# QKV projection on one Trainium2 core: the weight blocks of the first two row pairs in halves of K, and one x load at another place in ScalarE's order

## The chip, the cores and the metric

The kernel runs on one core of one Trainium2 chip. The metric is the device time of one execution in microseconds (us), the median of several executions. A profile is one execution recorded by the hardware profiler. Five engines work side by side[...]: PE (TensorE, matmuls; its weight loads are shown as PEld), DVE (VectorE), ACT (ScalarE), POOL (GpSimd) and SP (SyncE, which here only issues DMAs). SPq and ACTq are the DMA-issuing instructions of SP and ACT.

## The reference

```python
batch, seq, hidden = 16, 512, 768          # x: 16 x 512 x 768, w_qkv: 768 x 2304, fp32
qkv = np.matmul(x, w_qkv)                  # 8192 x 768 times 768 x 2304
q, k, v = qkv[..., :768], qkv[..., 768:1536], qkv[..., 1536:]
return np.stack([q, k, v], axis=0)         # 3 x 16 x 512 x 768, fp32
```

So it is one matrix product of 8192 rows with K = 768, cut into three outputs by columns.

## The kernel before

**Tiling.** The 8192 rows are taken in 32 pairs p = 0..31 of two row tiles of 128 rows (r = 0, 1). K = 768 is six slices of 128 (KT = 6), in two halves of three slices (KH = 3). The 2304 columns are five groups: two quads q = 0, 1 of two blocks c = 0, 1 of 512 columns (CB), and a remainder of 256 columns (`rem`, `w_rem`). All instructions stand in an order written out by hand: each engine runs its own instructions in the order in which the code emits them.

**Pairs 2 to 31** (`two`) use a scheme of the Strassen kind. For a quad, seven products of half the size replace eight. Products 1 and 2 are bf16 (`b1`, rows from `xb`), products 3 to 7 use fp32r sums of w (`t1` to `t4`, and the copy `b22`) and of x (`sr`, made on POOL by `sums_x`). The sums of w are made by DVE in `sum_w(q, n)`, once for each quad. `do(u, n)` multiplies product n and evicts it on ACT or adds it on DVE. In a pair the order on PE is: product 1 of both quads (a, b), then a2, a6, b2, b6, a5, a7, b5, b7, a4, rem, b4, a3, b3. Product 6 accumulates into the PSUM bank of product 1, so it can start only when ACT has evicted product 1 of that quad into its output tile `o`.

`early()`, in the middle of each pair, makes the next pair's operands: `transpose(p+1)` on DVE, `round_x` and `sums_x` on POOL, and the x load of pair p+2. `load_x(p, halves)` is four DMAs of 192 KB: half 0 is issued by SP (two of them), half 1 by ACT (two).

**Pairs 0 and 1** can't use the scheme yet, because the sums of w aren't made. They are multiplied directly, in bf16, block by block: `block(q, c, w, then)` runs over four row tiles n and calls `direct`, six matmuls that accumulate over all of K, then an eviction on ACT. Behind the evictions of n = 0 and of n = 1 the hook `then` puts the two casts (fp32 to bf16, ACT, one for each half of K) of the next block of w. The first block's halves are cast by DVE and ACT. The four blocks follow each other: (q, c) = (0,0), (0,1), (1,0), (1,1), with bf16 tiles `b1[0]`, `bt0`, `b1[1]`, `bt1`. `busy(n)` are matmuls on zeros that keep PE occupied during the head.

**Loads.** SP issues, in this order: rows of pair 0, w of the remainder (`str`), rows of pair 1, the blocks of quad 0 (`load_blocks(0, 0)` and `(0, 1)`: one DMA of 1536 KB each, fp32 tiles `st0`), half 0 of x of pair 2, the blocks of quad 1 (two DMAs of 768 KB for each, tiles `st1`), half 0 of x of pair 3. After that come the stores. ACT issues half 1 of x of pair 2 behind the first cast of `b1[0]`, and half 1 of x of pair 3 behind the evictions of block (0,0). A pool of eight large tiles (`big_pool`) holds first `str` and the four `st1` halves and later the output tiles `o`: an output tile of pair 2 comes free when the last reader of the `st1` half that lay there has finished. For quad 0 of pair 2 that reader is `sum_w(1, 1)`, for quad 1 it is `sum_w(1, 4)`.

The order on DVE in the head is: casts of the first rows, a half of `w_rem`, half a cast of `b1[0]`, `sum_w(0,1)`, `sum_w(0,2)`, `transpose(2)`, `sum_w(0,3)`, `sum_w(0,4)`, `b22[0]`, `sum_w(1,1)` to `sum_w(1,4)`, `b22[1]`, `transpose(3)`, and then the additions of pair 2.

Every DMA counts up one of eight completion semaphores, dealt out in turn; a DMA is issued only when the one before it on the same semaphore has landed.

Of the kernel before, what the change touches and what calls it, by code (L numbers as in the profile page):

```python
# [10 lines left out]
def kernel(  # L11
# [20 lines left out]
    nc = tc.nc  # L32
    P = 128
# [5 lines left out]
    KT = K // P  # L39
    KH = KT // 2  # L40
    KC = K // 4
    NP = M // (2 * P)
    CB = 512
    REM = N3 - 4 * CB
    Q_OFF = (0, 2 * CB + REM)
    R_OFF = 2 * CB
# [3 lines left out]
    ident = mybir.ActivationFunctionType.Identity  # L50
# [28 lines left out]

    def load_w(dst, j0, nj, off, cols):  # L80
        rows = w_qkv.rearrange("(p j) n -> p j n", j=KT)
        nc.sync.dma_start(dst[:], rows[:, j0:j0 + nj, off:off + cols])  # L82

    stage = {}

    def load_blocks(q, c):
        if q == 0:
            t = tq_pool.tile([P, KT, CB], fp32, name="st0", tag="tq")
            load_w(t, 0, KT, Q_OFF[q] + c * CB, CB)
            stage[q, 0, c], stage[q, 1, c] = t[:, :KH, :], t[:, KH:, :]  # L90
        else:
            for h in range(2):
                t = big_pool.tile([P, KH, CB], fp32, name="st1", tag="big")
                load_w(t, h * KH, KH, Q_OFF[q] + c * CB, CB)
                stage[q, h, c] = t[:]

    def sum_w(q, n):
# [9 lines left out]
    xin, xf, xb, sr = {}, {}, {}, {}  # L107
# [3 lines left out]
    def load_x(p, halves=(0, 1)):  # L111
        if p not in xin:
            xin[p] = xin_pool.tile([P, 2 * P // G, KC], fp32, name="xin")
        t = xin[p]
        rows = x_flat[p * 2 * P:(p + 1) * 2 * P, :].rearrange("(g b) k -> b g k", b=G)
        for n in range(2):
            for h in halves:
                i = 2 * h + n
                eng = (nc.sync, nc.scalar)[h]
                eng.dma_start(t[i * G:(i + 1) * G], rows[:, :, i * KC:(i + 1) * KC])  # L120
# [10 lines left out]
    def load_rows(p):  # L131
        xin[p] = xin_pool.tile([P, 2, K], fp32, name="xin")
        rows = x_flat[p * 2 * P:(p + 1) * 2 * P, :]
        nc.sync.dma_start(xin[p][:], rows.rearrange("(r m) k -> m r k", m=P))  # L134
# [37 lines left out]
    def quad(p, q):  # L172
        u = Quad()
        u.p, u.q = p, q
        u.o = big_pool.tile([P, 2, 2 * CB], fp32, name="o", tag="big")
        u.x = u.y = u.z = None
        return u
# [17 lines left out]
    def bank():  # L195
        return ps_pool.tile([P, CB], fp32, name="ps")
# [29 lines left out]
    def rows_of(s, p, lo, hi):  # L226
        return out_flat[s, p * 2 * P:(p + 1) * 2 * P, lo:hi].rearrange("(r m) n -> m r n", m=P)

    def store_quad(u):
        if u.q == 0:  # L230
            nc.sync.dma_start(rows_of(0, u.p, 0, H), u.o[:, :, :H])
            nc.sync.dma_start(rows_of(1, u.p, 0, 2 * CB - H), u.o[:, :, H:])
        else:
            part = 2 * H - Q_OFF[1]
            nc.sync.dma_start(rows_of(1, u.p, H - part, H), u.o[:, :, :part])
            nc.sync.dma_start(rows_of(2, u.p, 0, H), u.o[:, :, part:])
# [13 lines left out]
        nc.scalar.activation(o[:], ps[:], ident)  # L250
        nc.sync.dma_start(rows_of(1, p, R_OFF - H, R_OFF - H + REM), o[:])

    def direct(p, r, c, o, w):

        ps = bank()
        for j in range(KT):
            nc.tensor.matmul(  # L257
                ps[:], xb[p][:, j, r * P:(r + 1) * P], w[:, j, :],
                start=(j == 0), stop=(j == KT - 1),
            )  # L260
        nc.scalar.activation(o[:, r, c * CB:(c + 1) * CB], ps[:], ident)

    def two(a, b, early):

        do(a, 1)
        do(b, 1)
        early()
        do(a, 2)
        do(a, 6)
        do(b, 2)  # L270
        do(b, 6)
        do(a, 5)
        do(a, 7)
        do(b, 5)
        do(b, 7)
        do(a, 4)
        rem(a.p)
        do(b, 4)
        do(a, 3)
        store_quad(a)  # L280
        do(b, 3)
        store_quad(b)
# [49 lines left out]
    eye = w_pool.tile([P, P], fp32, name="eye")  # L332
    make_identity(nc, eye)
    st_rem = big_pool.tile([P, KT, REM], fp32, name="str", tag="big")
    load_w(st_rem, 0, KT, R_OFF, REM)
    load_rows(1)
    load_blocks(0, 0)
    load_blocks(0, 1)
    load_x(2, (0,))
    o0 = [quad(p, 0) for p in range(2)]  # L340
    load_blocks(1, 0)
    load_blocks(1, 1)
    load_x(3, (0,))
    o1 = [quad(p, 1) for p in range(2)]
# [7 lines left out]
    def cast(q, h, c, w, eng):  # L352

        dst = w[:, h * KH:(h + 1) * KH, :]
        if eng is nc.scalar:
            eng.activation(dst, stage[q, h, c], ident)  # L356
        else:
            eng.tensor_copy(out=dst, in_=stage[q, h, c])

    def block(q, c, w, then):  # L360

        for n in range(4):
            p, r = divmod(n, 2)
            direct(p, r, c, (o0, o1)[q][p].o, w)
            if c == 1 and r == 1:
                store_quad((o0, o1)[q][p])
            then(n)

    act, dve = nc.scalar, nc.vector
    busy(8)  # L370
# [11 lines left out]
    bt1 = bt_pool.tile([P, KT, CB], bf16, name="bt")  # L382
# [8 lines left out]

    def cast_next(q, c, w):

        return lambda n: n < 2 and cast(q, n, c, w, act)

    block(0, 0, b1[0], cast_next(0, 1, bt0))
    load_x(3, (1,))
    block(0, 1, bt0, cast_next(1, 0, b1[1]))
    block(1, 0, b1[1], cast_next(1, 1, bt1))
    block(1, 1, bt1, lambda n: None)  # L400
    t_1 = [tq_pool.tile([P, 2, KH, CB], f32r, name=f"t_1{n}", tag="tq") for n in range(2)]
    ts[1] = [t_1[n // 2][:, n % 2] for n in range(4)]
    for n in range(1, 5):
# [46 lines left out]
```

## Time and profile before

| what | us |
|---|---|
| device time, median of 5 runs (372.35 to 375.2) | 372.7 |
| device time of the profiled execution | 373.14 |
| span in the profile, first to last instruction | 371.4 |
| of the execution outside the span (373.14 - 371.4) | 1.7 |
| PE busy | 358.9 (97%) |
| DVE busy | 229.8 (62%) |
| ACT busy | 185.5 (50%) |
| POOL busy | 183.8 (50%) |
| start of pair 2 on PE | 39.86 |
| time of one pair from there on (54 matmuls) | 10.87 |

The busy time of PE is an average: from 39.86 us to the end PE has work all the time, and before that it waits several times. So the head, the first 40 us, has to be read by itself: the chain of work that ended last says what was on the path, the timeline of one engine shows each instruction with the wait ahead of it in brackets, and the view of waits adds them up. Landing times of the DMAs below are the last of the sixteen completion marks that the trace has for each DMA.

### The profile page before, as it was taken

To read this page: it belongs to the slowest core of one execution; us is meant where nothing else is said; L and a number is where in the kernel's file an instruction comes from. 1 tells how busy PE (TensorE), PEld (TensorE's weight loads), DVE (VectorE), ACT (ScalarE), POOL (GpSimd) and SP (SyncE) were. 2 spreads that over 40 slices of the span, in tenths; PEclk is the share of its full clock that TensorE was granted. 3 is DMA by queue.
4 is the path that set the end of the run, shared out by engine and by line. 5 is a ranking of instruction groups with operands and counts; after the bars stand their busy time and mean duration, and the time that the engine had idled before them with its cause. 6 is when DMAs were issued, how large, how long until landed. Compare 5 with 4: busy or idle time off the path is not lost.

```text
span 371.4 us, 5137 instructions
## 1 busy us (share of the span) xinstructions
PE 358.9 (97%) x1776; PEld 246.4 (66%) x1776; DVE 229.8 (62%) x227; ACT 185.5 (50%) x303; POOL 183.8 (50%) x186
## 2 busy tenths in 40 slices
PE   7887999999999999999999999999999999999994
PEld 4533566777676677767667766767776666777673
DVE  2289985556667555666655576664657666556732
ACT  3487554544445455444444544445454445545442
POOL 0019475665435566544456654445665444665510
PEclk9999999999999999999999999999999999999999
DMA  7999968899888899988888998888998988899776
GB/s 286 350 326 328 371 199 298 276 302 314 290 269 286 287 282 301 319 287 272 281 295 274 304 322 279 275 282 285 284 312 297 293 276 287 286 288 312 256 265 246
DMA packets 80906, 108.09 MB, mean 291 GB/s; under 512 B 4720, under 2 KB 60912, under 8 KB 80880
## 3 DMA queue, kind: packets, MB, share of 16 engines
q1 hardware_dynamic: 63984, 95.17, 78.6%
q10 hardware_dynamic: 16896, 12.59, 10.9%
q8 instruction: 14, 0.23, 0.3%
q14 instruction: 12, 0.10, 0.1%
HBM read 32.24 MB, written 75.50 MB: 290 GB/s over the span
## 4 chain that ended last, share of the span: by engine, by line
PE 89%; DMA 8%; SPq 1%; ACT 1%; issue 0%; ACTq 0%
PE ps L190 77%; PE ps L240 11%; DMA st<-in_w_qkv_dram 8%; PE ps L257 1%; ACT bt L356 0%; SPq L82 0%; SPq L134 0%; ACT orem L322 0%; ACTq L324 0%
## 5 line engine op out<-in xcount | busy, mean ns | idle before, releaser
L190 PE MATMUL ps<-t,s 128*128 128x512 f32 x720 | 194.4, 412 | 0.0
L190 PEld LDWEIGHTS ps<-t,s 128*128 128x128 f32 x720 | 133.1, 188 | 32.4 <-ACT o L217 0.4
L153 POOL CAST xb<-xf 128x1536 bf16<-128x1536 f32 x30 | 45.3, 1511 | 167.3 <-DVE xf L124 159.8
L124 DVE STREAM_TRANSPOSE xf<-xin 128x1536 f32<-128x1536 f32 x30 | 90.0, 3001 | 3.7 <-DMA xin<-in_x_dram 3.6
L190 PE MATMUL ps<-b,xb 128*128 128x512 bf16 x360 | 88.1, 381 | 0.0
L224 DVE TENSOR_TENSOR o<-o,ps 128x512 f32<-128x512 f32 x60 | 41.3, 688 | 61.7 <-PE ps L190 61.6
L218 DVE TENSOR_TENSOR o<-o,ps 128x512 f32<-128x512 f32 x60 | 41.2, 688 | 54.0 <-ACT o L217 54.0
L190 PEld LDWEIGHTS <-xb 128*128 128x128 bf16 x360 | 30.5, 98 | 44.5 <-issue 15.2
L217 ACT ACTIVATE o<-ps 128x512 f32<-128x512 f32 x60 | 35.9, 598 | 46.8 <-PE ps L190 46.8
L204 ACT ACTIVATE o<-ps 128x512 f32<-128x512 f32 x60 | 35.8, 597 | 44.7 <-PE ps L190 40.8
L211 ACT ACTIVATE o<-ps 128x512 f32<-128x512 f32 x60 | 35.9, 599 | 44.0 <-PE ps L190 43.9
L240 PE MATMUL ps<-w_rem,xb 128*128 128x256 bf16 x384 | 47.5, 273 | 1.0 <-DVE w_rem L373 1.0
L190 PE MATMUL ps<-b,s 128*128 128x512 f32 x180 | 46.5, 393 | 0.0
L240 PEld LDWEIGHTS <-xb 128*128 128x128 bf16 x384 | 35.2, 98 | 13.0 <-issue 9.4
L190 PEld LDWEIGHTS ps<-b,s 128*128 128x128 f32 x180 | 33.8, 188 | 8.0
L208 DVE TENSOR_TENSOR o<-o,ps 128x512 f32<-128x512 f32 x60 | 37.7, 671 | 2.0 <-PE ps L190 2.0
L221 ACT ACTIVATE o<-ps 128x512 f32<-128x512 f32 x60 | 35.9, 598 | 4.9 <-PE ps L190 0.4
L162 POOL TENSOR_TENSOR s<-s,xf 128x384 fp32r<-128x384 f32 x30 | 31.1, 1036 | 2.4
L165 POOL TENSOR_TENSOR s<-xf,s 128x384 fp32r<-128x384 f32 x30 | 32.0, 1066 | 0.0
L161 POOL TENSOR_TENSOR s<-xf 128x384 fp32r<-128x384 f32 x30 | 31.9, 1064 | 0.0
L163 POOL TENSOR_TENSOR s<-xf 128x384 fp32r<-128x384 f32 x30 | 31.7, 1056 | 0.0
L250 ACT ACTIVATE orem<-ps 128x512 f32<-128x512 f32 x31 | 18.5, 598 | 24.6 <-PE ps L240 24.6
(31 smaller groups left out, 110.9 us busy)
## 6 DMA issues: line engine op xcount, KB each, us to landing
out_dram<-o SPq DMA_DIRECT2D x62, 768.0 KB, 5.3
out_dram<-o SPq DMA_DIRECT2D x63, 256.0 KB, 4.9
xin<-in_x_dram SPq DMA_DIRECT2D x60, 192.0 KB, 6.7
xin<-in_x_dram ACTq DMA_DIRECT2D x60, 192.0 KB, 5.8
out_dram<-orem SPq DMA_DIRECT2D x31, 256.0 KB, 2.4
st<-in_w_qkv_dram SPq DMA_DIRECT2D x2, 1536.0 KB, 13.2
st<-in_w_qkv_dram SPq DMA_DIRECT2D x4, 768.0 KB, 15.5
xin<-in_x_dram SPq DMA_DIRECT2D x2, 768.0 KB, 6.0
```

Of the source, the lines that this page charges most:

```text
L124: nc.vector.transpose(t[:].rearrange("p j (g b) -> p g j b", b=G), xin.pop(p)[:].rearrange("p g (a j) -> p g j a", a=G),)
L153: nc.gpsimd.tensor_copy(out=xb[p][:], in_=xf[p][:])
L165: g.tensor_tensor(s[:, 4], a12, s[:, 2], op=sub)
L190: nc.tensor.matmul(ps[:], lhs[j], rhs[j], start=(start and j == 0), stop=(j == KH - 1), skip_group_check=True,)
L204: nc.scalar.activation(c11, u.x[:], ident)
L208: nc.vector.tensor_tensor(c11, c11, u.z[:], op=add)
L211: nc.scalar.activation(c12, u.x[:], ident)
L217: nc.scalar.activation(c22, u.x[:], ident)
L218: nc.vector.tensor_tensor(c22, c22, u.y[:], op=add)
L221: nc.scalar.activation(c21, u.x[:], ident)
L224: nc.vector.tensor_tensor(c12, c12, u.y[:], op=add)
L240: nc.tensor.matmul(ps, xb[p][:, j, r * P:(r + 1) * P], w_rem[:, j, :], start=(j == 0), stop=(j == KT - 1), skip_group_check=True,)
```

## The change

Three things are changed, all in the head of the kernel.

1. The blocks of quad 0 are loaded in two DMAs of 768 KB, one for each half of K, as those of quad 1 are already (`load_w` takes an access pattern in place of a tile for that).
2. `block` multiplies in halves: twelve matmuls of the first half of K over all four row tiles, in four PSUM banks, then twelve of the second half. The cast of the next block's first half stands on ACT ahead of the eviction of row tile 0, that of the second half ahead of the eviction of row tile 2. `direct` goes away.
3. Half 1 of the x load of pair 3, two DMAs on ACT's queue, stands behind block (1,0) where it stood behind block (0,0).

Lines of the changed kernel are one higher than before up to L251 (`sum_w` is L106, the evictions of `do` are L205 and so on); in the new `block` the matmul is L359 and the eviction L368, and the cast on ACT is L347.

```diff
-        nc.sync.dma_start(dst[:], rows[:, j0:j0 + nj, off:off + cols])
+        nc.sync.dma_start(dst, rows[:, j0:j0 + nj, off:off + cols])
...
             t = tq_pool.tile([P, KT, CB], fp32, name="st0", tag="tq")
-            load_w(t, 0, KT, Q_OFF[q] + c * CB, CB)
+            for h in range(2):
+                load_w(t[:, h * KH:(h + 1) * KH], h * KH, KH, Q_OFF[q] + c * CB, CB)
...
-    def block(q, c, w, then):
-
-        for n in range(4):
-            p, r = divmod(n, 2)
-            direct(p, r, c, (o0, o1)[q][p].o, w)
-            if c == 1 and r == 1:
-                store_quad((o0, o1)[q][p])
-            then(n)
+    def block(q, c, w, cast_next):
+
+
+        ps = [bank() for _ in range(4)]
+        for h in range(2):
+            for n in range(4):
+                p, r = divmod(n, 2)
+                for j in range(h * KH, (h + 1) * KH):
+                    nc.tensor.matmul(
+                        ps[n][:], xb[p][:, j, r * P:(r + 1) * P], w[:, j, :],
+                        start=(j == 0), stop=(j == KT - 1), skip_group_check=True,
+                    )
+                if h == 0:
+                    continue
+                if r == 0:
+                    cast_next(p)
+                o = (o0, o1)[q][p]
+                nc.scalar.activation(o.o[:, r, c * CB:(c + 1) * CB], ps[n][:], ident)
+                if c == 1 and r == 1:
+                    store_quad(o)
...
-        return lambda n: n < 2 and cast(q, n, c, w, act)
+        return lambda h: cast(q, h, c, w, act)
 
     block(0, 0, b1[0], cast_next(0, 1, bt0))
-    load_x(3, (1,))
     block(0, 1, bt0, cast_next(1, 0, b1[1]))
     block(1, 0, b1[1], cast_next(1, 1, bt1))
-    block(1, 1, bt1, lambda n: None)
+    load_x(3, (1,))
+    block(1, 1, bt1, lambda h: None)
```

More of the change, by code (lines that the diff above doesn't have):

```diff
@@ L93, in load_blocks @@
                 t = big_pool.tile([P, KH, CB], fp32, name="st1", tag="big")
-                load_w(t, h * KH, KH, Q_OFF[q] + c * CB, CB)
+                load_w(t[:], h * KH, KH, Q_OFF[q] + c * CB, CB)
                 stage[q, h, c] = t[:]
@@ L251, in rem @@
         nc.sync.dma_start(rows_of(1, p, R_OFF - H, R_OFF - H + REM), o[:])
[L253 to L261, printed above, removed]
     def two(a, b, early):
@@ L334 @@
     st_rem = big_pool.tile([P, KT, REM], fp32, name="str", tag="big")
-    load_w(st_rem, 0, KT, R_OFF, REM)
+    load_w(st_rem[:], 0, KT, R_OFF, REM)
     load_rows(1)
```

## The prediction

> **What bounds the kernel now.** First the page's chain of work that ended last: shares by engine, then by line.
>
> ```profile
> PE 89%; DMA 8%; SPq 1%; ACT 1%; issue 0%; ACTq 0%
> PE ps L190 77%; PE ps L240 11%; DMA st<-in_w_qkv_dram 8%; PE ps L257 1%; ACT bt L356 0%; SPq L82 0%; SPq L134 0%; ACT orem L322 0%; ACTq L324 0%
> ```
>
> PE is the path, except for 8% of loads of w. Where these lie is read from the same chain in order of time (start, length, what):
>
> ```profile
> 3.20 15.42 DMA st<-in_w_qkv_dram
> ...
> 18.64 15.13 DMA st<-in_w_qkv_dram
> ...
> 33.79 1.49 ACT bt L356
> ...
> 35.33 4.69 PE ps L257 x21
> 40.02 7.46 PE ps L190 x33
> 47.48 1.33 PE ps L240 x12
> ```
>
> So the head hangs on the last piece of w (landing 33.77), its cast, and 21 of the 24 matmuls of block (1,1). From 39.86 on PE never stops; only an earlier run through pair 2 can shorten the total. The waits of PE in the head:
>
> ```profile
> PE ps L257 <- ACT bt L356: 2.7, 3, 1.4
> PE ps L257 <- ACT b L356: 1.2, 1, 1.2
> PE ps L257 <- DVE b L358: 1.0, 1, 1.0
> ```
>
> That is 4.9 us, all for casts. This is what the change attacks. But before calling it a gain I ask what is late next, and take DVE's timeline:
>
> ```profile
> 23.63 2.99 DVE L124 STREAM_TRANSPOSE xf<-xin 128x1536 f32<-128x1536 f32 x1 [1.44 <-DMA xin<-in_x_dram]
> ...
> 39.71 2.55 DVE L105 TENSOR_TENSOR t<-st,t 128x1536 fp32r<-128x1536 f32 x1
> 42.18 0.95 DVE L405 CAST b<-st 128x1536 fp32r<-128x1536 f32 x1
> 43.05 3.08 DVE L124 STREAM_TRANSPOSE xf<-xin 128x1536 f32<-128x1536 f32 x1
> ```
>
> DVE waits for x of pair 2 until 23.63 and has no gap from there to 47 (19.44 us busy between 23.60 and 43.10). Its fourth sum for quad 1, `sum_w(1,4)` at 39.71, ends at 42.26. Who waits for it stands in ACT's and PEld's timelines:
>
> ```profile
> 42.37 0.60 ACT L204 ACTIVATE o<-ps 128x512 f32<-128x512 f32 x1 [1.02 <-DVE t L105]
> ...
> 43.02 4.03 PEld L190 LDWEIGHTS ps<-t,s 128*128 128x128 f32 x18 [0.19 <-ACT o L204]
> ```
>
> The output tile of quad 1 of pair 2 lies where the `st1` half lay that this sum reads last. So the eviction of b1 starts 0.1 us behind the sum, and b6, which accumulates into that bank, starts at 43.02. PE came to b6 at about 42.95: this second chain ends within 0.1 us of the first. **Two chains meet at b6**: w, casts, block (1,1), and x of pair 2, DVE. The change shortens the first alone.
>
> [...] the sums take 1.76 us ahead of POOL's start and 1.7 to 3.0 beside it, and POOL's x sums 1.6 to 2.5 against 1.0 later. So DVE's chain is long by its own order with POOL, which the change leaves alone. [...] between 19 and 22 us ACT's queue moved 334 packets of 768 B and SP's 299 of 2 KB. [...] The trace shows only that it fell 4.2 us after the last matmul (370.7 against 366.5); no gap in the kernel reaches 1.5 us.
>
> **The change part by part.** Matmuls of 512 columns follow each other every 0.2158 us, so twelve take 2.59. A cast takes 1.48 on ACT, 0.96 on DVE; an eviction 0.52 in a row.
>
> *Halved loads of quad 0* (two more DMAs on SP, no byte more). 1536 KB took 9.49 to 13.55 = 4.06, so the first half lands at about 11.5. DVE is free at 11.61, casts to 12.57; PE starts when `busy(4)` ends, 13.42 instead of 14.60. The second half lands at 13.55 as now, cast to 15.06, needed at 16.0. Block (0,0) ends at 18.6.
>
> *Block (0,1)*: first half landed about 15.6, cast to 17.1; second landed 18.62, cast to 20.1, needed at 21.2. Ends 23.8 (now 26.6).
>
> *x load moved.* It puts 0.39 MB on ACT's queue between 21.3 and 32.0, beside the last three pieces of w, which need 10.2 us (23.55 to 33.77) where three times 2.03 would do. Its second DMA also held ACT until 23.62 (1.12 us, `ACT o L261 <- DMA xin`). Without it the last piece lands earlier by 1.0 us (its bytes at the 390 GB/s of 5 to 15 us) to 2.5; I take 2.3: landings 26.9, 29.0, 31.4.
>
> *Blocks (1,0) and (1,1).* Piece one lands at 23.55, cast to 25.03, matmuls 25.1 to 27.7; piece two cast 26.9 to 28.4, matmuls to 31.0; piece three cast behind two evictions, 29.4 to 30.9, matmuls to 33.6; piece four 31.95 to 33.4, matmuls to 36.2 instead of 39.86. **PE reaches pair 2 earlier by 3.65 us**, or by 2.0 if the moved load frees nothing. The change in `block` does most of it: behind the last cast twelve matmuls remain, not 21. Four banks at once cost nothing: two blocks use eight, and each block's banks are evicted before the next but one begins.
>
> *What is late next.* a1, b1, a2 (nine matmuls), a6, b2 bring PE to b6 at about 39.5. It waits there until the eviction behind `sum_w(1,4)`: 42.26 + 0.1 + 0.6 = 43.0. Queued behind the waiting eviction on ACT are the x loads of pair 4 and a6's eviction, neither late: both start there today too. So PE stands for some 3.5 us and then goes on as now. The 4.9 us of waits in the head turn into one wait at b6.
>
> *Does DVE's chain move?* Its two sums of quad 0 end at 20.4 rather than 22.2, but transpose(2) waits for x of pair 2, whose last part (ACT's queue, issued behind the cast at 13.58, landed 23.60) is issued by the same instruction at the same time, and the order of bytes on SP's queue ahead of it is the same. So: zero. Bounds: if x landed the moment DVE is free, 23.6 - 20.4 = 3.2 us sooner. The other way, the trace has a 16 KB packet of the instruction queue at 24.4 that took 1.10 us on one DMA engine, where the next landing then trailed by 1.8. If it goes with PE's place in the program, it moves to 21 to 22.5, into the landing of x: up to 1.1 late. I take 0.3 us late, between no delay and that bound.
>
> *The moved load's own user.* transpose(3) stands at 43.05. The load is now issued behind the evictions of row tiles 2 and 3 of block (1,0), at about 34.2, and ACT's x loads took 5.3 to 9.1 us: landing 40 to 43.5. Its second DMA waits for the first remainder store, which is issued at about 22.5 and lands by 33. transpose(3) may slip to 44.25 free: the c22 additions behind it end at 47.9 and a3, which needs the first, starts at 49.1; xb of pair 3 has 3.1 us. At a landing of 44.9 (9.1 plus a w 1.6 later) it would cost 0.7.
>
> Sum: the profiled execution's 373.14, less 0, plus 0.3 = 373.4. The median stands 0.4 below that execution, so **373.0 us** for a median. 0.5% (1.9 us) is about what a measurement of this kernel can tell from no change.
>
> **The rivals.**
>
> *1. The gain comes through (faster).* For it: 4.9 us of waits at casts, gone. Against: the wait of ACT on `t L105`, which doesn't depend on blocks. It needs x of pair 2 sooner; at most the 3.2 us above, 372.7 - 3.2 = 369.5; half of it gives 371.1. Chance of over 0.5%: 0.09.
>
> *2. The new wait cools the clock (slower).* [...] Against: the 4.2 us that the clock held at the end of this trace. Chance 0.08.
>
> *3. x of pair 3 lands late (slower).* From a landing of 44.25 every us costs one at a3; at 46.5 it is 2.3 us, 375.3. For it: full DMA queues (1.04 to 1.08 of the engines to 43 us) and 2 MB of stores ahead. Chance of over 0.5%: 0.05.
>
> *4. The change doesn't do what it says*: the casts still stop PE. By the bound above PE then comes to b6 at 41.1, and the total is the same.
>
> **How the numbers follow.** Forecast and rival 4 (b6 where it is, within 1.9 us): 0.77; faster 0.09; slower 0.14 (rivals 2 and 3, and 0.01 for what I don't see). The likeliest case alone spans 372.4 (no delay and a fast median) to 373.8 (1.1 late). With part of both sides the range is 371.0 to 375.0: below lies the upper half of rival 1, above most of rivals 2 and 3.
>
> **What would show it.** Right: PE's matmuls of `block` end near 36 us; waits of PE on casts under 2 us in the head; a gap of about 3.5 us on PE ahead of b6, ended by ACT's eviction (L205), which waits for DVE's sum (L106); DVE without a gap from 23.6 to 46. Moved load: landing between 40 and 43.5. Wrong: b6 starting before 42 (x of pair 2 came early, or the tile lies elsewhere), a granted clock of half around 43 to 47 us, or transpose(3) waiting for x past 44.25.

## The result, and the profile after

The changed kernel takes 375.55 us (median of 43 executions, 371.87 to 379.02) beside 372.91 us (median of 80, 372.07 to 376.06) for the kernel before. The ratio is 1.0039 [1.0024, 1.0054]: slower by 0.4%, or 1.4 us, where the forecast was 0.3 us. The ratios here are of means without the executions that are over 1.5% above the fastest of their kernel; that takes out 13 of the 43 and none of the 80, and with all of them counted the means, like the medians, lie 2.6 us apart. The profiled execution of after took 377.93 us (span 376.1), near the upper end of the range, so a second trace of the same kernel (`after_again`, 374.06 us, span 372.3) stands beside it below.

**The chain of work that ended last**, shares by engine, then by line:

```profile
PE 86%; DMA 9%; SPq 2%; DVE 1%; issue 1%; ACT 0%; ACTq 0%; DVEq 0%
PE ps L191 76%; PE ps L241 10%; DMA xin<-in_x_dram 7%; DMA out_dram<-o 2%; SPq L82 1%; DVE t L106 1%; SPq L135 0%; ACT orem L313 0%; ACT o L205 0%; ACTq L315 0%; DVEq L209 0%; ACTq L205 0%; SPq L121 0%; DVEq L125 0%
```

`DMA st<-in_w_qkv_dram`, 8% before, is gone from it, and `DVE t L106`, the sums of w, is in it: the chain now comes through DVE. The x loads and the store that the view puts ahead of that sum are not what held it. DVE's timeline has no gap from 26.30 us to it, so the path goes back along DVE to the transpose that waited for x of pair 2.

**The waits of PE in the head**, from 12 to 62 us (us in total, times, longest):

```profile
PE ps L191 <- ACT o L205: 5.2, 1, 5.2
PE ps L359 <- ACT b L347: 2.0, 1, 2.0
```

Three rows of waits for casts, 4.9 us, have become one of 2.0, and a new one of 5.2 has come for an eviction: the gap at b6. ACT's timeline has that eviction, with what it waited for:

```profile
45.03 0.60 ACT L205 ACTIVATE o<-ps 128x512 f32<-128x512 f32 x1 [6.31 <-DVE t L106]
```

**PE's timeline** shows where it lies (start, length, what, and in brackets the wait ahead of it):

```profile
26.32 5.34 PE L359 MATMUL ps<-b,xb 128*128 128x512 bf16 x24 [1.95 <-ACT b L347]
31.50 5.40 PE L359 MATMUL ps<-bt,xb 128*128 128x512 bf16 x24
36.73 2.10 PE L191 MATMUL ps<-b,xb 128*128 128x512 bf16 x9
38.86 0.94 PE L191 MATMUL ps<-t,s 128*128 128x512 f32 x3
39.64 0.82 PE L191 MATMUL ps<-b,xb 128*128 128x512 bf16 x3
45.68 6.56 PE L191 MATMUL ps<-t,s 128*128 128x512 f32 x18 [5.21 <-ACT o L205]
```

Pair 2 starts at 36.73 instead of 39.86. Its b6 starts at 45.68 instead of 43.02, and the 18 matmuls from there take 6.56 us.

**DVE's timeline** gives the reason for the late start of b6:

```profile
26.30 2.99 DVE L125 STREAM_TRANSPOSE xf<-xin 128x1536 f32<-128x1536 f32 x1 [4.57 <-DMA xin<-in_x_dram]
...
42.37 2.54 DVE L106 TENSOR_TENSOR t<-st,t 128x1536 fp32r<-128x1536 f32 x1
44.84 0.95 DVE L408 CAST b<-st 128x1536 fp32r<-128x1536 f32 x1
45.70 2.99 DVE L125 STREAM_TRANSPOSE xf<-xin 128x1536 f32<-128x1536 f32 x1
```

Each of these stands some 2.7 us later than its line before (23.63, 39.71, 42.18, 43.05). DVE waited 4.57 us for x of pair 2, which landed 2.5 us later than before, and `sum_w(1,4)` ends late by about that.

**PE by windows** of 3.41 us, at the borders where the granted clock changes (stretch, its length, PE busy and matmuls, PEclk, DMA share, GB/s; PEclk is the granted clock as a share of full), gives the reason for the 6.56:

```profile
36.70:40.12 3.42, 3.40 (x16) 1.00 1.08 393
40.12:43.53 3.41, 0.35 (x2) 1.00 1.04 407
43.53:46.94 3.41, 1.26 (x3) 0.50 0.76 235
46.94:50.35 3.41, 3.41 (x9) 0.50 0.29 61
```

The window busy for 0.35 us was followed by one at half clock, and the one busy for 1.26 by another. At full clock the 18 matmuls took 4.41 to 4.51 us (4.46 before), so 2.1 us are lost. Late start and clock together, 2.66 + 2.1 = 4.8, are the 4.7 us by which the span grew (371.4 to 376.1).

### The profile page after: what moved, and what is told of

The parts are those of the page before. It is cut to its first block, busy times and chain, and to the rows that moved or that the text cites. A ratio compares the mean times of both kernels' runs of the same rounds, so it can differ in the third digit from the quotient of the medians.

```text
span 376.1 us, 5142 instructions
## 1 busy us (share of the span) xinstructions
PE 361.1 (96%) x1776; PEld 248.2 (66%) x1776; DVE 229.6 (61%) x227; ACT 185.4 (49%) x303; POOL 183.9 (49%) x186
## 4 chain that ended last, share of the span: by engine, by line
PE 86%; DMA 9%; SPq 2%; DVE 1%; issue 1%; ACT 0%; ACTq 0%; DVEq 0%
PE ps L191 76%; PE ps L241 10%; DMA xin<-in_x_dram 7%; DMA out_dram<-o 2%; SPq L82 1%; DVE t L106 1%; SPq L135 0%; ACT orem L313 0%; ACT o L205 0%; ACTq L315 0%; DVEq L209 0%; ACTq L205 0%; SPq L121 0%; DVEq L125 0%
## 5 line engine op out<-in xcount | busy, mean ns | idle before, releaser
L191 PE MATMUL ps<-t,s 128*128 128x512 f32 x720 | 196.4, 415 | 5.2 <-ACT o L205 5.2
L191 PEld LDWEIGHTS ps<-t,s 128*128 128x128 f32 x720 | 134.6, 191 | 38.8 <-ACT o L205 5.7
L219 DVE TENSOR_TENSOR o<-o,ps 128x512 f32<-128x512 f32 x60 | 41.2, 687 | 57.6 <-ACT o L218 57.6
L205 ACT ACTIVATE o<-ps 128x512 f32<-128x512 f32 x60 | 35.8, 597 | 50.6 <-PE ps L191 42.2
L251 ACT ACTIVATE orem<-ps 128x512 f32<-128x512 f32 x31 | 18.5, 598 | 24.6 <-PE ps L241 24.6
```

The costliest lines, as they stand in the source:

```text
L191: nc.tensor.matmul(ps[:], lhs[j], rhs[j], start=(start and j == 0), stop=(j == KH - 1), skip_group_check=True,)
L205: nc.scalar.activation(c11, u.x[:], ident)
L219: nc.vector.tensor_tensor(c22, c22, u.y[:], op=add)
```

## The experiments

Two quantities from the trace are used in all of them. **Lag**: in many traces of either kernel some early loads have one of their sixteen completion marks well behind the others. I take it from `str`, the load of w for the remainder, as last mark less ninth. It was 0.1 to 1.7 us and goes with no edit. Half 1 of x of pair 2 (x2 from here) is issued by ACT behind a cast that waits for w, so the lag delays it. **Trail**: the last mark of x2's last DMA, less the mark before it. All times are of the profiled execution; `packet` is the start of the 16 KB packet on PE's instruction queue that comes nearest to x2.

| trace | lag | packet | trail | x2 landed | b6 | half clock | span |
|---|---|---|---|---|---|---|---|
| before | 0.34 | 24.38 | 0.24 | 23.60 | 43.02 | none | 371.4 |
| after | 0.81 | 22.71 | 1.18 | 26.11 | 45.68 | 43.53 to 50.35 | 376.1 |
| after_again | 0.21 | 22.10 | 0.81 | 24.43 | 43.97 | 25.82 to 29.23 | 372.3 |
| e_fill | 1.18 | 23.14 | 1.34 | 26.70 | 46.26 | 47.28 to 50.69 | 376.2 |
| e_sum4 | 1.70 | 23.15 | 1.30 | 27.56 | 44.66 | 44.06 to 50.89 | 375.8 |
| e_x_back | 0.12 | 21.86 | 0.13 | 23.45 | 42.99 | 44.48 to 47.90 | 372.9 |
| e_x2 | 0.12 | 23.14 | – | 21.97 | 42.05 | 27.84 to 31.25 | 370.4 |
| e_x2_sum4 | 0.42 | 23.39 | – | 22.54 | 39.70 | none | 369.2 |
| e_b_sum4 | 0.16 | 23.58 | 0.05 | 22.97 | 43.46 | 29.69 to 33.10 | 371.8 |
| e_x_only | 1.18 | 26.12 | 0.01 | 25.25 | 44.67 | 46.12 to 49.53 | 374.6 |
| e_half_loadsb | 1.63 | 23.69 | 0.90 | 26.99 | 46.52 | 30.70 to 34.12 | 374.8 |
| e_b_x2_sum4b | 0.14 | 25.01 | – | 21.98 | 43.06 | none | 371.5 |
| e_fetch_lateb | 0.17 | 24.14 | 0.02 | 23.89 | 43.42 | 44.09 to 47.50 | 373.3 |
| e_b_fetch_earlyb | 1.53 | 22.49 | 1.19 | 27.63 | 47.04 | 47.03 to 50.44 | 376.9 |

(A half clock after the last matmul of the kernel is left out; `e_sum4` has one more at 9.93 to 13.34. In the three rows with a dash x2's half 1 is no longer the last to land; the landing is that of half 0.)

Two things hold over the whole table. In the nine traces that keep the order of the sums and the place of x2's issue, **b6 starts 19.41 to 19.57 us after x2 has landed**. And the span is 371.4, plus b6 less 43.02, plus what the 18 matmuls from b6 take over 4.45 us: 1.5 us with one window at half clock behind b6, 2.1 and 2.8 with two. It comes out within 0.2 us in every row but that of `e_x2_sum4`, told below.

**after_again**: the changed kernel once more, no edit.

> The changed kernel once more, for its spread and for a second look at the landing of x of pair 2. Theory (two chains meet at b6): PE is at b6 near 40 us and waits for the eviction behind the fourth sum of quad 1[...]. Time 372 to 379, middle near 375; b6 starts 2.6 us after the start of DVE's first sum-free wait ends, that is about 19.4 us after x of pair 2 has landed. Rival A (the clock alone): b6 starts at 43.0 as before and all that is lost is lost at half clock. Rival B (the moved x load): transpose(3) waits for x of pair 3.

Median 376.76 (before, beside it, 374.49), ratio 1.0034 [1.0006, 1.0061]. The wait at b6, 5.2 us in the profiled execution, was 2.4 here. In this trace x2 landed 0.83 us late, b6 came 0.95 late, and the span is 0.9 longer. PE's timeline and windows:

```profile
43.97 4.41 PE L191 MATMUL ps<-t,s 128*128 128x512 f32 x18 [2.39 <-ACT o L205]
```

```profile
22.41:25.82 3.41, 1.34 (x7) 1.00 1.04 358
25.82:29.23 3.41, 2.89 (x7) 0.50 1.06 367
39.47:42.88 3.41, 2.12 (x10) 1.00 1.04 379
42.88:46.30 3.42, 2.33 (x10) 1.00 1.04 242
```

The gap at b6, 2.4 us, fell across a border of two windows, which left each of them busy for 2.1 us or more, and the clock held. A half clock did come at 25.82, in `block`, but there it cost nothing: PE still had to wait at b6. So what this trace lost, it lost to the late x alone.

**e_fill**: 14 matmuls on zeros ahead of b6 of pair 2, to keep PE busy in the gap.

```diff
+        if fill:
+            busy(fill)
```

> The changed kernel with 14 matmuls on zeros (3.0 us) put on PE between b2 and b6 of pair 2; nothing else moves. Theory: [...] the granted clock stays at 0.998 or more, and what remains over the kernel before is the lateness of DVE's chain alone: 372.7 + 0 to 2.7, about 373.7. Rival A (the clock is all): 372.7. Rival B (the moved x load): as the changed kernel, about 375.

Median 376.75, ratio 1.0046 [1.0020, 1.0072], so no better. The zeros ran from 40.88 to 44.07, but x2 landed at 26.70 in this execution, 2.2 us of the gap remained, and the granted clock was 0.50 from 47.28 all the same: 14 matmuls were too few for a gap with x this late. As a test of the clock the trace is inconclusive, but the executions say something. Five of the 22 had a mean clock of 0.997 or more, so no half clock before the end, and they took 373.74 to 376.87 us, median 375.99; the 43 executions of before with such a clock beside them have a median of 373.94. So some 2 us can be lost without the clock. The zeros may be up to 1.1 of them, since they end at 44.07 and b6 could start at 43.0 with x on time.

**e_x_back**: the x load of pair 3 at its old place, the rest as changed.

```diff
 block(0, 0, b1[0], cast_next(0, 1, bt0))
+load_x(3, (1,))
...
-load_x(3, (1,))
```

> The changed kernel with half 1 of the x load of pair 3 back behind block (0,0), the halved loads and blocks kept. Theory: the last piece of w lands 1 to 2.3 us later than in the changed kernel, PE comes to b6 at 41 to 42, the gap falls to 1 to 4 us; x of pair 2 and DVE's chain stay as in the changed kernel: 372.7 to 375, the clock whole in most runs. Rival B (the moved x load costs the time): back to 372.7, and b6 at 43.0.

Median 375.91, ratio 1.0033 [1.0008, 1.0057]: as slow as the full change, where a whole clock in most runs was expected; 3 of 22 had one, and took 373.04 to 373.97 us. In its trace x2 was not late (23.45), b6 starts at 42.99 as before, and yet the span is 1.5 us longer. Here the clock stands alone:

```profile
42.99 5.99 PE L191 MATMUL ps<-t,s 128*128 128x512 f32 x18 [1.98 <-ACT o L205]
```

```profile
37.66:41.07 3.41, 3.35 (x16) 1.00 1.05 401
41.07:44.48 3.41, 1.49 (x6) 1.00 1.04 366
44.48:47.90 3.42, 3.42 (x10) 0.50 1.07 221
```

The gap of 2.0 us lies inside one window and leaves it busy for 1.49 us of 3.41, and the next one ran at half clock: 5.99 less 4.45 is the 1.5. The change is as slow without the moved x load. That load does move w: the last piece landed at 33.40 here and at 31.78 in `after_again`, at nearly the same lag.

**e_sum4**: `sum_w(1, 4)`, which frees the tile for b6, ahead of `sum_w(1, 3)`, in the changed kernel.

```diff
-    for n in range(1, 5):
+    for n in (1, 2, 4, 3):
```

> The changed kernel with the sums of quad 1 in the order 1, 2, 4, 3, so that the last reader of the buffer of b's output tile is the third sum, not the fourth. Theory: the eviction of b1 is released one sum (2.0 us) sooner, b6 starts 2.0 us sooner than in the changed kernel (41.0 with x of pair 2 on time, 43.7 if it is 2.7 late), the gap is 1.5 to 4 us, the clock falls in few runs: 371 to 373.5. Rival A: the gap is shorter, so no half clock, but b6 at 43.0: 372.7. Rival B, or if something other than this buffer holds b6: as the changed kernel, about 375.

Median 372.85 (before 374.49), ratio 0.9971 [0.9941, 1.0002]. The profiled execution is one with a long lag (1.70) and two windows at half clock, 377.62 us, but b6 starts 17.1 us after x2 instead of 19.5: releasing b6 sooner does move it. The gap is shorter, not gone.

**e_x2**: x2's half 1 issued by ACT ahead of the casts of the first block, in the changed kernel.

```diff
     rem(0)
+    load_x(2, (1,))
...
-    load_x(2, (1,))
```

> The changed kernel with half 1 of the x load of pair 2 issued earlier on ACT: behind the eviction of the first remainder (about 10 us) in place of behind the cast that waits for the first block of w (13.4 to 15.7 us, as late as that block lands). Theory (b6 starts 19.4 us after x of pair 2 has landed, and what is lost beyond that is half clock): x of pair 2 then lands with half 0, at 20.5 to 22.5, DVE's chain starts 1.5 to 4 us sooner than in the changed kernel, b6 at 40.5 to 42, PE's gap there falls to 0.5 to 2 us, hardly any half clock behind it: 371 to 372.5 where the kernel before takes 373 to 374.5, and little spread. Rival A (the clock alone): PE's gap at block (1,0), 2 to 3 us, is left, so the clock falls as often: no change from the changed kernel. Rival C (the fourth sum is bound by w, not by x): b6 stays.

Median 373.94 (before 374.58), ratio 0.9995 [0.9972, 1.0017], where some 2 us less than before was expected. x2 landed at 21.97, b6 has no gap, and the span of the trace is 370.4. But w came later in turn: PE waited 3.3 us for a cast of `b1[1]` (before this edit 2.0 and 2.6), the granted clock was 0.50 from 27.84, behind a window busy for 0.94 us, and `block` ended at 38.9. With the chain from x2 over DVE (chain 2) shortened, the one from w over the casts and blocks (chain 1) sets b6 again.

**e_x2_sum4**: both edits in the changed kernel.

> Both: x of pair 2 earlier as in e_x2, and the sums of quad 1 in the order 1, 2, 4, 3. Theory: b6 is released at 38.5 to 40, before PE comes to it (about 39.6), so the first chain (w, casts, blocks) bounds the head at last and the change's gain appears: 2.5 to 3.3 us less than the kernel before, 369.5 to 371, with whole clock behind b6. Rivals: as the changed kernel or as e_sum4 alone.

Median 371.94 (370.36 to 372.86; before 374.58), ratio 0.9927 [0.9900, 0.9954]: **faster than both kernels**, by 0.7% against before. PE's timeline, DVE's, and the waits of PE:

```profile
36.59 2.11 PE L191 MATMUL ps<-b,xb 128*128 128x512 bf16 x8
38.34 1.05 PE L191 MATMUL ps<-t,s 128*128 128x512 f32 x3
39.23 0.82 PE L191 MATMUL ps<-b,xb 128*128 128x512 bf16 x3
39.70 4.50 PE L191 MATMUL ps<-t,s 128*128 128x512 f32 x18
```

```profile
34.45 4.41 DVE L106 TENSOR_TENSOR t<-st,t 128x1536 fp32r<-128x1536 f32 x2
38.78 2.56 DVE L106 TENSOR_TENSOR t<-st,st 128x1536 fp32r<-128x1536 f32 x1
```

```profile
PE ps L191 <- DVE o L219: 0.9, 1, 0.9
```

The sum that releases b6 ends at 38.9, so b6 starts at 39.70 with no gap, 3.3 us sooner than before, at full clock. Of the 3.3 us, 1.1 is given back in pair 2: 0.9 where PE waits for DVE's addition L219, behind `transpose(3)`, which is the next bound. The span is 2.2 us shorter.

**e_b_sum4** and **e_b_x2_sum4b**: the order of the sums alone, and both edits, in the kernel before (the diffs above).

> The kernel before with the sums of quad 1 in the order 1, 2, 4, 3 and nothing else. Theory: in the runs in which x of pair 2 is on time, PE came to b6 at 42.95 anyway, so nothing is gained (372.3 to 372.7); in runs in which it lands late, up to 2 us are: the median falls by 0 to 1.5 us and the spread shrinks. Against the rival that this order is a gain of 2 us by itself, whatever the blocks do.

> The kernel before (blocks and w loads as before) with both edits of e_x2_sum4: half 1 of x of pair 2 issued earlier, sums of quad 1 in the order 1, 2, 4, 3. Theory: with b6 released before PE comes to it, the first chain bounds the head, and PE comes to b6 at 42.9 as in the kernel before: 372 to 372.7, little spread, and 2 to 3 us more than e_x2_sum4. That difference is what the halved blocks are worth once the second chain is out of the way. Rival D (the halved blocks are worth nothing, the two edits are all of it): as e_x2_sum4, 370.4 to 372.9.

Ratios 1.0000 [0.9977, 1.0022] and 1.0004 [0.9982, 1.0026]. b6 starts at 43.46 and 43.06, both times as soon as PE comes to it, with no wait. The second trace:

```profile
43.06 4.51 PE L190 MATMUL ps<-t,s 128*128 128x512 f32 x18
```

In the kernel before a free b6 is worth nothing, because chain 1 is as long. So the change does earn 0.7%, but only in company with an earlier release of b6; neither side has any gain alone. How much of the 0.7% is the halves and how much the moved load was not tested.

**e_x_only**: the x load moved, nothing else, in the kernel before. **e_half_loadsb**: only the loads of quad 0 in halves, in the kernel before.

```diff
-            load_w(t, 0, KT, Q_OFF[q] + c * CB, CB)
+            for h in range(2):
+                load_w(t[:, h * KH:(h + 1) * KH], h * KH, KH, Q_OFF[q] + c * CB, CB)
```

> The kernel before with the x load of pair 3 moved behind block (1,0), blocks and loads as before. Theory: the last piece of w lands 1 to 2.3 us sooner (31.5 to 32.8 with x of pair 2 on time), block (1,1) ends at 37.7 to 39, PE waits for b6, which stays 19.4 us behind the landing of x of pair 2: the kernel before, or up to 1.7 us slower through half clock. Rival B (the moved load is what costs): as the changed kernel, 2 us slower, with transpose(3) waiting for x of pair 3.

> The kernel before with the two blocks of quad 0 loaded in halves, the blocks multiplied as before. Asked: why x of pair 2 lands later in the changed kernel at equal lateness of the loads ahead of it (its last part trails the middle of its sixteen marks by 1.2 to 1.5 us there, by 0.2 to 0.6 in the kernels with the old blocks). Theory F (the 16 KB instruction packet of PE, which goes with PE's place in the program and comes 2 us sooner where PE is faster, falls into that landing): here PE is as before, the packet comes at about 24 and the trail is 0.2 to 0.6. Rival G (the two more DMAs and their changed semaphores): the trail is 1.2 to 1.5. Time as the kernel before.

The moved load alone: 1.0003 [0.9962, 1.0044], with a median over all 13 executions of 376.33 beside 374.58, so that it costs nothing is not shown. It has a pattern: of the 13 executions the five with a mean clock of 0.998 or more took 372.07 to 373.31 us, the eight with 0.989 to 0.994 took 375.65 to 378.39. The halved loads alone: 1.0043 [0.9998, 1.0087] over 7 executions, which does not settle whether they cost anything. The traced one had a lag of 1.63. Its last mark came 1.4 us behind the middle of the sixteen, as rival G expected; but x2 landed so late there (26.99) that the packet, at 23.69, came well ahead of it, so this does not tell G from theory F.

**e_fetch_lateb** and **e_b_fetch_earlyb** ask why x2 has a trail with the change and none without. The packet on PE's instruction queue comes at the same place of PE's program in all traces, behind 93 to 105 matmuls. The first takes ten zero matmuls out of the changed kernel, so that this place is reached later; the second puts narrow ones for wide ones in the kernel before, so that it is reached sooner.

```diff
 # changed kernel, fetch later
-    busy(8)
+    busy(1)
...
-    busy(4)
+    busy(1)
 # kernel before, fetch earlier
-    busy(8)
+    busy(4, 16)   # 16 more of 64 columns
```

> The changed kernel with one matmul on zeros in place of eight at the start, and one in place of four ahead of block (0,0): 20 PE instructions less ahead of the 16 KB instruction packet. Theory F: the packet comes some 2 us later in time (24 or more), behind the landing of x of pair 2, whose trail falls to 0.2 to 0.6 us. Rival G: the trail stays at 1.2 to 1.5. PE starts with half clock, so the time is not what is asked.

> The kernel before with four matmuls on zeros and sixteen short ones in place of eight at the start: 24 PE instructions more ahead of the 16 KB instruction packet, in about the same time. Theory F: the packet comes at 20.5 to 22 us rather than 24, into the landing of x of pair 2, whose trail grows to 1.2 to 1.5 us, and the time by about 1 us against a run with as punctual loads. Rival G: the trail stays at 0.2 to 0.6.

These are one execution each, 375.09 and 378.70 us. PE does start slower in the first: its first twelve transposes take 2.82 us, where they took 1.85 before. (In the trace of before the eight zero matmuls at the start follow each other every 0.427 us, the four at 12.56 every 0.216. The granted clock is on record only from 5.46 us on, at 1.00.) The packets belong to this line of the profile's DMA queues (packets, MB, share of 16 engines), here of after:

```profile
q8 instruction: 14, 0.23, 0.3%
```

The packet moved as meant, to 24.14 in the changed kernel (from 22.10 at a like lag) and to 22.49 in the kernel before (from 24.38). Where it starts after x2 has landed, x2's last mark trails by 0.01 to 0.24 us: before, `e_b_sum4`, `e_x_only`, and now the changed kernel too, with 0.02. Where it starts ahead of the landing, one mark of sixteen trails by 0.81 to 1.34 us: four traces of the changed kernel, `e_half_loadsb`, and now the kernel before, with 1.19. The packet takes 1.10 to 1.21 us. So the trail goes with the packet and not with the kernel, and rival G falls: `e_b_fetch_earlyb` has a trail without the two more DMAs, `e_fetch_lateb` has them and no trail. `e_b_fetch_earlyb` shows less of the packet than it was built for, since at its lag of 1.53 x2 landed at 27.63, which an unmoved packet would have preceded too. The marks of the other loads give a cleaner test. In the six traces with a lag of up to 0.21 no load that landed ahead of the packet has a trail over 0.14, and the first piece of w to land behind it has one of 1.1 to 2.1. One trace disagrees as to x2: `e_x_back` has the packet at 21.86, ended 0.4 us ahead of the landing, and a trail of 0.13, while its next piece of w trails by 1.10. Why x2 escaped there is open.

`e_fetch_lateb` shows again that this is not all. Its b6 is only 0.4 us late, the gap is 3.6 us, the granted clock is 0.50 from 44.09, and the span is 1.9 longer.

## Why the prediction was right, and where it was not

**Right: what bounds the kernel, and that the gain stops at b6.** Two chains met there and the change shortened one. `block` ended at 36.7 us in the profiled execution (forecast 36.2; 38.1 in `after_again`, where the clock fell in `block`), the waits for casts went from 4.9 us to 2.0 (2.6 in `after_again`; forecast under 2), and the gap at b6 is ended by L205 behind L106. The test of "change shortens the first alone" is the pair `e_b_x2_sum4b` and `e_x2_sum4`: with b6 released the same change is worth 0.7%. Rival 1 was rightly small, since x came no sooner.

**Right: the moved load.** Its own user never waited: it landed at 40.34, inside 40 to 43.5, and `transpose(3)` started straight behind DVE's work. Rival 3 is false. The 2.3 us for the last piece of w measured 1.6 (33.40 to 31.78); it shows no effect on the total (1.0034 and 1.0033 with and without the move).

**Mis-sized: the 0.3 us in "Does DVE's chain move?"** The mechanism was named: the instruction packet moves from 24.4 to about 22 with PE's place and into x2's landing. It was bounded at 1.1 and taken at 0.3. It measured 0.81 to 1.34 in four of the traces of the changed kernel that leave x2's issue in its place, and about nothing in two. In the profiled execution it is 0.94 of the 2.5 us (a trail of 1.18 against 0.24). The rest goes for the most part with the lag, 0.81 against 0.34: x2's issue was 0.42 later, and the mark before the last came 1.14 later after it. With a lag of 0.8 or more that mark comes 10.4 to 10.9 us after the issue, in traces of either kernel's tiling. At a small lag it takes 9.1 to 9.4 with the tiling of before and 9.6 to 9.8 in the changed kernel, so some half a microsecond may be the change's own. Before, too, has executions with such a lag: its range, up to 376 us, has room for them.

**Failed: the chance of rival 2, the clock.** The 0.08 was an estimate of mine: when the clock falls was not shown. All that the trace of before has is a clock that held for 4.2 us behind the last matmul and then fell to 0.50, and a head in which it held through waits of up to 1.4 us. The later traces show more. Every half clock ahead of the last matmul lasts 3.41 us or twice that, and in the profiled execution the two falls, at 43.53 and, behind the last matmul, at 374.62, lie 331.09 us apart, which is 97 times 3.413. So I take a grid of such windows, laid through eleven traces from 12 us on. Behind every window at full clock with PE busy for up to 1.34 us (eight of them) it fell; of six with 1.41 to 1.57 us it fell behind three (1.44, 1.49, 1.53) and held behind three (1.41, 1.46, 1.57); with 2.12 us and more it held every time. In the three traces that keep their clock (`before`, `e_x2_sum4`, `e_b_x2_sum4b`; grid laid from the half clock behind their last matmul) no window was busy for less than 1.66 us. So in these traces the border lies near 1.5 us, 44% of a window. Some records of matmuls are missing (`e_x2_sum4` shows eight of the nine at 36.59), which may be why the middle is mixed. By that border, an estimate from these windows alone, a gap of 1.9 us is enough where it lies in one window (`e_x_only`: 1.88 us, busy for 1.53, then 0.50), and one of 3.5 leaves one of the two windows that it touches at least half idle, which is close to the border at best. The mean clock of the executions shows how often a window at half clock comes anywhere ahead of the end, not only at b6. A window at half clock takes 0.5 x 3.41 / 375 = 0.0045 off the mean, and 0.997 or more means none. That holds for 79 of 136 executions of before that ran beside the experiments, one of 66 of the changed kernel, 8 of 11 of `e_x2_sum4`. One of the signs named for being wrong, a half clock around 43 to 47 us, is what the profiled execution has. One window at half clock behind b6 cost 1.5 to 1.6 us: the 18 matmuls took 5.98 to 6.02 us in four traces, 4.46 before.

**Together.** The forecast, 0.3 us slower, was 1.1 us short of the measured 1.4 (2.3 short with every execution counted), in the direction of rival 2, whose chance of 0.08 was far too low. By the ratio the changed kernel stands at some 374.2 us, inside the range of 371.0 to 375.0; its median over all executions, 375.55, lies above it. That the ratio falls inside is in part luck: the range took in most of rivals 2 and 3 at its upper end, but the likeliest case ended at 373.8. How the loss is shared between late x and clock is not settled, since every median mixes executions with and without either. `e_x_back`, 1.0033 with a trace that has the clock's loss alone, speaks for the clock as the larger part; the five executions of `e_fill` with a whole clock and a median of 375.99 speak for the late x.

## What to carry to other kernels

Where two chains end at one instruction, find both before you shorten one. Here the change alone cost 0.4%, the two edits that release b6 gave nothing alone (1.0004), and all together gave 0.7%. A wait that is merged out of several short ones need not be neutral for TensorE: in the trace of before the granted clock stayed at 1.00 through several waits of up to 1.4 us, and in `e_x_back` it was 0.50 behind one of 2.0 us. When a load decides, look at all sixteen completion marks: one mark that trails by a microsecond asks another question than sixteen late ones.

## What the runs showed of the hardware that I had not expected

- The granted clock of TensorE was 0.50 behind all eight windows of 3.41 us at full clock in which PE was busy for 0.35 to 1.34 us, and behind three of the six with 1.41 to 1.57. None of these windows was without a matmul. It was 1.00 again after 3.41 us in most of the traces, after 6.83 in two.
- The fetch of PE's instructions that falls into the head, one packet of 16 KB, took 1.10 to 1.21 us, and loads that landed behind its start had one mark of sixteen late: x2 by 0.81 to 1.34 us in six traces of seven, the next piece of w by 1.1 to 2.1 in the six traces with a small lag. What delayed that one mark was not shown: the trace does not name the DMA engine that took the packet. With more or fewer matmuls ahead the packet moved, from 24.38 to 22.49 and from 22.10 to 24.14.
- One mark of an early load was late by 0.1 to 1.7 us from execution to execution, with no edit behind it. By way of the one cast that ACT does ahead of x2's issue it moved the start of b6: by 1.65 us in `e_x_only`, at a lag of 1.18 and with no trail. Why it is late no run here shows.
